# Two decoder layers on one core: memory queries produced in columns, their sums of squares on the tensor engine, and a last product cut in two

## The chip, the cores and the metric

The kernel runs on one core of a Trainium2 chip. The metric is the device time of one execution in microseconds; the time of a kernel is the median of several runs. The core's engines are named as in the profile: PE multiplies matrices, PEld is PE's loading of its stationary operand, DVE and ACT do elementwise work and reductions, POOL is a slower engine for small work, SP issues DMAs. PE writes only into PSUM, eight banks of 512 fp32 columns by 128 partitions; ACT and DVE carry results from there to SBUF.

## What is computed

Two layers over 256 positions of width 1024. With `h = RMSNorm(x)`, each layer multiplies `h` by one 1024 x 5120 matrix whose columns feed three branches and a gate:

```python
q_a, k_a, v_a, q_h, f_h, i_h, q_m, z = jnp.split(proj, split_points, axis=-1)
...
kv_m = rms_norm(mem, mem_norm_g[l]) @ w_mem_kv[l]
...
qm = rms_norm(q_m.reshape(B, S, MEM_HEADS, MEM_HEAD_DIM), mem_q_norm[l])
o_m = memory_attention(qm, km, vm).reshape(B, S, G)
...
y = jnp.concatenate([o_a, o_h, o_m], axis=-1) * jax.nn.silu(z)
x = x + y @ w_out[l]
```

Branch A is causal softmax attention (8 heads of 64), branch H a gated linear recurrence (4 heads of 128), branch M attention of the 256 positions to 256 memory tokens (4 heads of 128). The change is in branch M's queries `q_m`: each head's 128 channels are normalised by their root mean square before the scores with the memory keys.

## The kernel before

Weights come in chunks of 128 x 1024 fp32 (512 KB), one DMA each on SP. Each chunk is split in two reduced-precision parts, `wh` (a cast on ACT, L143) and `wl` (the rest, a subtraction on DVE, L158); activations are split likewise (`hTh`, `hTl`). Each product is then three matmuls: high by high, and the two mixed ones.

The projection goes column group by column group of 512. There are two forms. `group_b` (L204) holds 128 positions of the normalised input stationary and moves 512 weight columns: the result has positions on partitions and channels along the row; it is 8 x 2 x 3 = 48 matmuls of 512 columns into two PSUM tiles. `group_a` (L263) holds 128 weight columns stationary and moves the 256 positions: the result is transposed, channels on partitions and positions along the row; it is 4 x 8 x 3 = 96 matmuls of 256 columns, two of the four column blocks sharing a PSUM tile. A layer does the memory keys and values (`group_kv`), then FH and QH (`group_a`), KA, QA, IH, ZH (`group_b`), ZA and ZM (`group_a`), QM and VA (`group_b`), and then the output projection (`w_out_phase`), whose 12 row blocks of 24 matmuls are taken in the order H, A, M.

In `group_kv`, and in ZH's group in layer 0 alone, the very last matmul of 512 columns is issued as one of 384 and one of 128 (`pieces`, L215).

Everything else is written as generators that run beside this stream: `slot` (L189) steps all of them once, eight times per group, and what they emit mixes with the projection's matmuls. The final order on each engine comes from a scheduler that simulates the program when it is built; instructions handed to `pin` (L119) keep their program order on their engine, and `tc.issue_after` puts an instruction behind a named one. PSUM holds four `acc` tiles for the projections and four `sd` tiles for the generators; `held`, `room`, `take` and `rel` (L61 to L82) count who holds which buffer.

`g_qm` (L1132) takes QM's two tiles (positions on partitions): ACT copies them to `qm` (L1136) and squares them, DVE sums the squares of each head along the row (`sumsq`, L588); `rsq` (L593) makes the reciprocal roots `r` on DVE and POOL, and L1141 their negative `nr`. Then, for each half of the positions, four transposes on PE (L1150) turn the queries to channels on partitions, and ACT and DVE split them into `qmh` and `qml` (L1151, L1152). Two `g_mem_unit`s follow, two heads each: scores into two `sd` tiles (L1171), maxima on DVE, exponentials on ACT with bias `nr` times the maximum and scale `r` (L1186), division on DVE, transposes (L1205), products with the values, and the gated result for the output projection.

`g_moba_unit` (L1030) is branch A, two units a layer. After its exponentials (L1076) and the division, the three column blocks of `P` are transposed, four heads each (L1095), into three `sd` tiles, and copied to `PT` by ACT (L1096). The blocks go in the order 0, 1, 2; block 0 needs only the first half of the positions. When both units are there and VA is done, L1116 multiplies by the values.

The host lays the weights out in the order of the chunks: groups of `group_a` by column blocks, the others by row blocks (`tiles`, L1346).

Of the kernel before, what the change touches and what calls it, by code (L numbers as in the profile page):

```python
# [12 lines left out]
F32 = mybir.dt.float32  # L13
# [5 lines left out]
OP = mybir.AluOpType  # L19
# [27 lines left out]
def hymba_kernel(ctx: ExitStack, tc: tile.TileContext, front, x, x_t, mem, mem_t, positions, w_in, w_out, w_mem_kv,  # L47
# [57 lines left out]
    for l in range(DEPTH):  # L105
# [3 lines left out]
        for c in (KA, QA, IH, ZH, ZA, ZM, QM, VA):  # L109
            (add_a if c in (ZA, ZM) else add_b)(w_in, base + c * G * D)  # L110
# [86 lines left out]
    def mm(o, a, b, s, e):  # L197
        nc.tensor.matmul(o, lhsT=a, rhs=b, start=s, stop=e)  # L198
# [64 lines left out]
    def group_a(thl, each):  # L263

        for h in range(4):
# [4 lines left out]
            for k in range(8):  # L270
# [3 lines left out]
                mm(o, wL, thl[:, k, 0], False, k == 7)  # L274
                if k == 3:
                    slot(False)
            st["c"] += 1
# [378 lines left out]

    lbs = cst.tile([128, 2, 4], F32, name="lbs")
# [299 lines left out]
    def g_qk(l, q, acc):  # L957
# [41 lines left out]
        if q:  # L999
            k2 = [sb.tile([128, n], F32R, name="k2", tag=t, bufs=1)[:, n - 2048 - o:n - o].rearrange(  # L1000
                "p (h c s) -> p h c s", h=4, c=2) for t, n, o in (("k2", 2112, 48 * l), ("y2", 2048, 0))]
# [28 lines left out]
    def g_moba_unit(l, u):  # L1030
# [57 lines left out]
        yield from take(tag)  # L1088
        PT = sb.tile([128, 4, 384], F32, name="PT", tag=tag, bufs=1)
        for b in range(3):  # L1090
# [3 lines left out]
            for i in (3, 2, 1, 0):  # L1094
                pin(nc.tensor.transpose(pt[:, i * 128:(i + 1) * 128], P[:, i, bs], ident))  # L1095
# [3 lines left out]
        T[f"PT{u}"] = PT  # L1099
        if u == 0:  # L1100
            return
# [30 lines left out]
    def g_qm(l, acc):  # L1132
        ss = small("ssq", 8)
        qm = sb.tile([128, 2, 512], F32, name="qm", tag="qk", bufs=1)
        for t in range(2):
            nc.scalar.copy(qm[:, t], acc[t])  # L1136
        for t in range(2):
            sumsq(ss[:, t * 4:t * 4 + 4], acc[t], 4)
# [3 lines left out]
        yield 2  # L1142
        qmh = sb.tile([128, 4, 256], F32R, name="qmh", tag="ih", bufs=1)
        qml = sb.tile([128, 1088], F32R, name="qml", tag="hF", bufs=1)[:, 16:1040].rearrange("p (k s) -> p k s", k=4)
        for t in range(2):
            ts = slice(t * 128, (t + 1) * 128)
            yield from room("sd")
            pt = side_tile()
            for h in range(4):
                nc.tensor.transpose(pt[:, h * 128:(h + 1) * 128], qm[:, t, h * 128:(h + 1) * 128], ident)  # L1150
            nc.scalar.copy(qmh[:, :, ts], heads(pt, 4))  # L1151
            nc.vector.tensor_tensor(qml[:, :, ts], heads(pt, 4), qmh[:, :, ts].bitcast(F32), op=OP.subtract)  # L1152
            rel()
# [236 lines left out]
```

## Time and profile before

| | |
|---|---|
| median of 3 runs | 394.92 us (394.49 to 395.57) |
| the profiled execution's own time | 395.92 us |
| its span, first to last instruction | 394.1 us |
| mean granted TensorE clock | 0.999 |
| moved from and to HBM | 67.27 MB read, 1.05 MB written |
| transposes of the memory queries (L1150) | 16, two runs of four in each layer |
| transposes of branch A (L1095) | 48, 12 for each of 4 units |

The span is what the trace covers; the time of an execution holds it and a little around it. A timeline line gives the start in us, the length in us, the engine, the source line, the operation, what it writes and reads, the shapes, and how many neighbours of one kind were merged into it (x). Matmuls overlap: the length of one reaches into the next, so the distance from one start to the next is what one takes. A line can be a helper's: all plain matmuls are L198, all pinned narrow ones L202.

### The profile page before, as it was taken

The page shows a single profiled execution, that of the slowest core. Times are in us where ns is not written, and L with a number is a line of the kernel's source. Part 1 is how long each engine was busy: PE and PEld are TensorE (multiplying, and loading weights), DVE is VectorE, ACT ScalarE, POOL GpSimd, SP SyncE. Part 2 cuts the span into 40 slices and gives each one's busy share as a digit, 9 for nine tenths or more (in the row PEclk, how much of TensorE's full clock was granted, in tenths as well). Part 3 has the DMA queues.
Part 4 walks back from the last instruction along what each step waited for, and adds up shares of the span by engine and source line. Part 5 has one row for each costly group of instructions (what it writes and reads, how often), then busy time and mean ns, then how long its engine had stood idle before and what let it go on. Part 6 is the DMA issues. An engine that isn't in the chain of part 4 may idle for free.

```text
span 394.1 us, 7915 instructions
## 1 busy us (share of the span) xinstructions
PE 389.2 (99%) x3053; PEld 352.3 (89%) x3053; DVE 314.8 (80%) x632; ACT 255.9 (65%) x411; POOL 68.1 (17%) x94
## 2 busy tenths in 40 slices
PE   8999999999999999999999999999999999999996
PEld 5889988888999888999988999888889998899996
DVE  3799989999895777876586999799999684588563
ACT  5878867438757999644463876445685974968330
POOL 2005925531001002000061030033400200200000
PEclk9999999999999999999999999999999999999999
DMA  8988664549754363533656375636674266444203
GB/s 261 419 337 278 217 215 148 174 124 236 191 200 161 108 224 116 172 129 108 201 171 198 133 229 192 215 108 215 190 221 153 80 190 204 143 159 161 76 33 108
DMA packets 22662, 70.93 MB, mean 180 GB/s; under 512 B 2528, under 2 KB 5984, under 8 KB 22624
## 3 DMA queue, kind: packets, MB, share of 16 engines
q1 hardware_dynamic: 19872, 67.86, 52.3%
q10 hardware_dynamic: 2752, 2.56, 2.7%
q8 instruction: 24, 0.39, 0.4%
q14 instruction: 14, 0.11, 0.1%
HBM read 67.27 MB, written 1.05 MB: 173 GB/s over the span
## 4 chain that ended last, share of the span: by engine, by line
PE 97%; DMA 2%; SPq 0%; ACT 0%; issue 0%; DVE 0%; DVEq 0%
PE acc L198 61%; PE acc L1243 17%; PE sd L198 11%; PE sd L202 2%; DMA mw<-in_front_dram 2%; PE sd L1116 1%; PE sd L1095 1%; PE sd L1010 1%; PE sd L1205 1%; PE sd L1150 0%; PE sd L771 0%; PE sd L635 0%; SPq L123 0%; PE sd L424 0%; ACT wh L148 0%; ACT mTh L351 0%
## 5 line engine op out<-in xcount | busy, mean ns | idle before, releaser
L143 ACT CAST wh<-wr 128x1024 fp32r<-128x1024 f32 x104 | 108.7, 1052 | 72.3 <-PE acc L198 40.1
L158 DVE TENSOR_TENSOR wl<-wr,wh 128x1024 fp32r<-128x1024 f32 x104 | 126.2, 1219 | 24.2 <-PE acc L1243 8.0
L198 PE MATMUL acc<-wh,hT 128*128 128x512 f32 x385 | 121.1, 392 | 0.0
L198 PE MATMUL acc<-hT,wh 128*128 128x256 f32 x512 | 89.7, 278 | 0.0
L198 PEld LDWEIGHTS acc<-wh,hT 128*128 128x128 f32 x385 | 72.0, 188 | 14.7
L198 PEld LDWEIGHTS acc<-hT,wh 128*128 128x128 f32 x512 | 77.6, 188 | 0.2
L198 PE MATMUL acc<-wl,hT 128*128 128x512 f32 x192 | 75.5, 393 | 0.0
L198 PE MATMUL acc<-hT,wl 128*128 128x256 f32 x256 | 70.6, 278 | 0.0
L198 PEld LDWEIGHTS acc<-hT,wl 128*128 128x128 f32 x256 | 47.9, 188 | 0.0
L198 PEld LDWEIGHTS acc<-wl,hT 128*128 128x128 f32 x192 | 36.1, 188 | 7.0
L1243 PE MATMUL acc<-yh,wl 128*128 128x256 f32 x128 | 35.6, 279 | 0.0
L1243 PE MATMUL acc<-yl,wh 128*128 128x256 f32 x128 | 35.3, 277 | 0.0
L1243 PE MATMUL acc<-yh,wh 128*128 128x256 f32 x128 | 35.0, 279 | 0.0
L1243 PEld LDWEIGHTS acc<-yl,wh 128*128 128x128 f32 x128 | 24.1, 188 | 0.1
L1243 PEld LDWEIGHTS acc<-yh,wl 128*128 128x128 f32 x128 | 24.1, 188 | 0.0
L161 DVE SCALAR_TENSOR_TENSOR wl<-wr,gT,wh 128x1024 fp32r<-128x1024 f32 (+1 forms) x14 | 19.1, 1374 | 6.0 <-PE acc L1243 1.9
L1243 PEld LDWEIGHTS acc<-yh,wh 128*128 128x128 f32 x128 | 23.8, 188 | 0.1
L148 ACT ACTIVATE wh<-wr,gT 128x1024 fp32r<-128x1024 f32 (+1 forms) x14 | 15.2, 1089 | 11.4 <-PE acc L198 5.1
L1243 PE MATMUL acc<-y,wh 128*128 128x256 f32 x128 | 21.8, 276 | 0.0
L1243 PEld LDWEIGHTS acc<-y,wh 128*128 128x128 f32 x128 | 19.2, 188 | 0.0
L1243 PE MATMUL acc<-y,wl 128*128 128x256 f32 x64 | 17.5, 276 | 0.0
L1076 ACT ACTIVATE P<-P,nba,rq 128x128 f32<-128x128 f32 (+1 forms) x32 | 17.2, 540 | 0.1
(250 smaller groups left out, 675.0 us busy)
## 6 DMA issues: line engine op xcount, KB each, us to landing
wr<-in_w_in_dram SPq DMA_DIRECT2D x80, 512.0 KB, 3.7
wr<-in_w_out_dram SPq DMA_DIRECT2D x24, 512.0 KB, 3.5
wr<-in_w_mem_kv_dram SPq DMA_DIRECT2D x12, 512.0 KB, 3.3
k<-k ACTq DMA_DIRECT2D x8, 256.0 KB, 6.3
zT<-in_x_dram SPq DMA_DIRECT2D x2, 512.0 KB, 9.1
xs<-in_x_t_dram SPq DMA_DIRECT2D x2, 512.0 KB, 9.8
memr<-in_mem_dram SPq DMA_DIRECT2D x2, 512.0 KB, 5.3
mw<-in_front_dram SPq DMA_DIRECT2D x2, 384.0 KB, 6.3
```

Source lines behind the costliest of these rows:

```text
L143: ins = nc.scalar.copy(whs[i], raws[i])
L148: nc.scalar.activation(whs[i][:, sl], raws[i][:, sl], AF.Copy, scale=gT[:, g:g + 1])
L158: nc.vector.tensor_tensor(wls[i], raws[i], whs[i].bitcast(F32), op=OP.subtract)
L161: nc.vector.scalar_tensor_tensor(wls[i][:, sl], in0=raws[i][:, sl], scalar=gT[:, g:g + 1], in1=whs[i][:, sl].bitcast(F32), op0=OP.mult, op ...
L198: nc.tensor.matmul(o, lhsT=a, rhs=b, start=s, stop=e)
L202: tc.keep_in_program_order(nc.tensor.matmul(o, lhsT=a, rhs=b, start=True, stop=True))
L1010: nc.tensor.transpose(pt[:, p * 128:(p + 1) * 128], kr[:, t, p * 128:(p + 1) * 128], ident)
L1076: pin(nc.scalar.activation(P[:, i, kc[t]], P[:, i, kc[t]], AF.Exp, bias=nb[:, c:c + 1], scale=rq[:, r:r + 1], accum_out=sm[:, c:c + 1]))
L1095: pin(nc.tensor.transpose(pt[:, i * 128:(i + 1) * 128], P[:, i, bs], ident))
L1116: pin(nc.tensor.matmul(po[w][rows, c + o:c + 256], lhsT=va[:, b, h * 64:(h + 1) * 64], rhs=PT[e][:, p, 256 * b:256 + 128 * b], start=b == ...
L1205: nc.tensor.transpose(pt[:, i * 256 + t * 128:i * 256 + (t + 1) * 128], P[:, t, i, b * 128:(b + 1) * 128], ident)
L1243: ins = nc.tensor.matmul(a, lhsT=wt, rhs=y, start=first and (to is not None or b % 2 == 0), stop=n == nk - 1 and j == 2, skip_group_check= ...
```

## The change

It has four parts. The memory queries' projection (QM) goes through `group_a` instead of `group_b`, in both layers, so they arrive with channels on partitions: the eight transposes are gone, `qmh` and `qml` are written straight from the projection's tiles, and the host lays QM's weights out as for `group_a`. The sums of squares now run over partitions and are made on PE: `ones32`, 128 x 32 ones, is the stationary operand, and four products, one for each 32 positions of a half, fill the four quarters of the partitions of an `sd` tile, for each pair of heads. DVE multiplies by `m32`, which keeps of each 32 equal rows' columns the own position, and sums, so that the result has positions on partitions, as before. These products wait until the second unit of branch A has emitted its transposes.

In `g_moba_unit` the blocks are transposed in the order 1, 2, 0; in layer 0 the first unit waits until the third column block of QM's group has been issued, and its transposes stay behind that block's last matmul (`T["last"]`). The transposes of the memory units (L1205) are pinned.

The split of the last 512-column matmul in 384 and 128 applies to ZH's and VA's groups of both layers. And the tile `k2` has the same place in its buffer in both layers.

```diff
         for c in (KA, QA, IH, ZH, ZA, ZM, QM, VA):
-            (add_a if c in (ZA, ZM) else add_b)(w_in, base + c * G * D)
+            (add_a if c in (ZA, ZM, QM) else add_b)(w_in, base + c * G * D)
...
-    def group_a(thl, each):
+    def group_a(thl, each, name=None):
...
-                mm(o, wL, thl[:, k, 0], False, k == 7)
+                last = nc.tensor.matmul(o, lhsT=wL, rhs=thl[:, k, 0], start=False, stop=k == 7)
                 if k == 3:
                     slot(False)
+            T["last"] = last.ins
+            done.add((name, h))
...
+    m32 = cst.tile([128, 32], F32, name="m32")
+    ones32 = cst.tile([128, 32], F32, name="ones32")
+
+    def g_m32():
+        nc.vector.memset(ones32, 1.0)
+        nc.vector.tensor_reduce(m32, ident.rearrange("p (g s) -> p s g", g=4), AX.X, OP.add)
         yield
...
             k2 = [sb.tile([128, n], F32R, name="k2", tag=t, bufs=1)[:, n - 2048 - o:n - o].rearrange(
-                "p (h c s) -> p h c s", h=4, c=2) for t, n, o in (("k2", 2112, 48 * l), ("y2", 2048, 0))]
+                "p (h c s) -> p h c s", h=4, c=2) for t, n, o in (("k2", 2112, 0), ("y2", 2048, 0))]
...
         yield from take(tag)
+        while u == l == 0 and ("qm0", 2) not in done:
+            yield
         PT = sb.tile([128, 4, 384], F32, name="PT", tag=tag, bufs=1)
-        for b in range(3):
+        for b in (1, 2, 0):
...
             for i in (3, 2, 1, 0):
-                pin(nc.tensor.transpose(pt[:, i * 128:(i + 1) * 128], P[:, i, bs], ident))
+                with tc.issue_after(T["last"]) if u == l == 0 else nullcontext():
+                    pin(nc.tensor.transpose(pt[:, i * 128:(i + 1) * 128], P[:, i, bs], ident))
...
+        done.add(("pt", 2 * l + u))
...
-    def g_qm(l, acc):
+    def g_qm(l, h0, acc):
+        if h0 == 0:
+            T["qm"] = (sb.tile([128, 4, 256], F32R, name="qmh", tag="ih", bufs=1),
+                       sb.tile([128, 1088], F32R, name="qml", tag="hF", bufs=1)[:, 16:1040].rearrange(
+                           "p (k s) -> p k s", k=4))
+            T["q2"] = []
+        qmh, qml = T["qm"]
+        hs, a = slice(h0, h0 + 2), heads(acc, 2)
+        nc.scalar.copy(qmh[:, hs], a)
+        sq = sb.tile([128, 512], F32, name="sq", tag="sq", bufs=2)
+        nc.scalar.activation(sq, acc, AF.Square)
+        T["q2"].append(sq.rearrange("p (h t g s) -> p h t g s", h=2, t=2, g=4))
+        nc.vector.tensor_tensor(qml[:, hs], a, qmh[:, hs].bitcast(F32), op=OP.subtract)
+        if h0 == 0:
+            return
+        while ("pt", 2 * l + 1) not in done:
+            yield
+        yield from room("sd")
+        pt = side_tile()
+        for u, sq in reversed(list(enumerate(T.pop("q2")))):
+            for g in range(4):
+                mm_row(pt[g * 32:g * 32 + 32, u * 128:u * 128 + 128], ones32, sq[:, :, :, g])
         ss = small("ssq", 8)
-        qm = sb.tile([128, 2, 512], F32, name="qm", tag="qk", bufs=1)
-        for t in range(2):
-            nc.scalar.copy(qm[:, t], acc[t])
-        for t in range(2):
-            sumsq(ss[:, t * 4:t * 4 + 4], acc[t], 4)
+        sd = sb.tile([128, 512], F32, name="sq", tag="sq", bufs=2)[:, :256]
+        nc.vector.tensor_tensor(sd.rearrange("p (a s) -> p a s", s=32), pt[:, :256].rearrange("p (a s) -> p a s", s=32),
+                                m32[:, None, :].to_broadcast([128, 8, 32]), op=OP.mult)
+        nc.vector.tensor_reduce(ss.rearrange("p (t h) -> p h t", t=2), sd.rearrange("p (h t s) -> p h t s", t=2, s=32),
+                                AX.X, OP.add)
+        rel()
         r = rsq("qm", ss, 8, 128)
         nr = small("nrm", 8)
         nc.gpsimd.tensor_scalar(nr, r, -1.0, None, op0=OP.mult)
-        yield 2
-        qmh = sb.tile([128, 4, 256], F32R, name="qmh", tag="ih", bufs=1)
-        qml = sb.tile([128, 1088], F32R, name="qml", tag="hF", bufs=1)[:, 16:1040].rearrange("p (k s) -> p k s", k=4)
-        for t in range(2):
-            ts = slice(t * 128, (t + 1) * 128)
-            yield from room("sd")
-            pt = side_tile()
-            for h in range(4):
-                nc.tensor.transpose(pt[:, h * 128:(h + 1) * 128], qm[:, t, h * 128:(h + 1) * 128], ident)
-            nc.scalar.copy(qmh[:, :, ts], heads(pt, 4))
-            nc.vector.tensor_tensor(qml[:, :, ts], heads(pt, 4), qmh[:, :, ts].bitcast(F32), op=OP.subtract)
-            rel()
         yield 2
...
-                    nc.tensor.transpose(pt[:, i * 256 + t * 128:i * 256 + (t + 1) * 128],
-                                        P[:, t, i, b * 128:(b + 1) * 128], ident)
+                    pin(nc.tensor.transpose(pt[:, i * 256 + t * 128:i * 256 + (t + 1) * 128],
+                                            P[:, t, i, b * 128:(b + 1) * 128], ident))
...
+    spawn(g_m32(), 40)
...
+            elif gen is g_qm:
+                group_a(hT, lambda h, a: g_qm(l, h, a), f"qm{l}")
             else:
-                acc = group_b(hTh, hTl, gen is g_zh and not l)
+                acc = group_b(hTh, hTl, gen in (g_zh, g_va))
...
-            if c in (FH, QH, ZA, ZM):
+            if c in (FH, QH, ZA, ZM, QM):
```

More of the change, by code (lines that the diff above doesn't have):

```diff
@@ L1129, in g_moba @@
             yield 4
-    def g_qm(l, acc):
-        ss = small("ssq", 8)
-        qm = sb.tile([128, 2, 512], F32, name="qm", tag="qk", bufs=1)
-        for t in range(2):
-            nc.scalar.copy(qm[:, t], acc[t])
-        for t in range(2):
-            sumsq(ss[:, t * 4:t * 4 + 4], acc[t], 4)
+    def g_qm(l, h0, acc):
[14 more added lines that the diff above has]
+        while ("pt", 2 * l + 1) not in done:
+            yield
+        yield from room("sd")
[3 more added lines that the diff above has]
+                mm_row(pt[g * 32:g * 32 + 32, u * 128:u * 128 + 128], ones32, sq[:, :, :, g])
+        ss = small("ssq", 8)
+        sd = sb.tile([128, 512], F32, name="sq", tag="sq", bufs=2)[:, :256]
[4 more added lines that the diff above has]
+        rel()
         r = rsq("qm", ss, 8, 128)
```

## The prediction

> **What bounds the kernel now.** I read the page first: busy time by engine, then the chain that ended last, then the timeline of PE around the places that the change touches.
>
> ```profile
> PE 389.2 (99%) x3053; PEld 352.3 (89%) x3053; DVE 314.8 (80%) x632; ACT 255.9 (65%) x411; POOL 68.1 (17%) x94
> ...
> PE 97%; DMA 2%; SPq 0%; ACT 0%; issue 0%; DVE 0%; DVEq 0%
> ```
>
> PE is busy for 389.2 of 394.1 us, and 97% of the chain is PE following PE. So the time is a sum of what each PE instruction costs. Busy PE is not proof of a full PE, so I price an instruction by the distance from its start to the next start, in the timeline (start us, us, engine, line, what). First the two products that carry the kernel, 512 columns and 256 columns wide, where nothing interrupts them:
>
> ```profile
> 330.36 0.62 PE L198 MATMUL acc<-wh,hT 128*128 128x512 f32 x2
> ...
> 331.04 0.62 PE L198 MATMUL acc<-wh,hT 128*128 128x512 f32 x2
> ...
> 374.04 0.28 PE L1243 MATMUL acc<-yl,wh 128*128 128x256 f32 x1
> ...
> 374.38 0.28 PE L1243 MATMUL acc<-yl,wh 128*128 128x256 f32 x1
> ```
>
> Three 512s start between 330.36 and 331.04, 0.68 us, 0.227 each; three 256s between 374.04 and 374.38, 0.34 us, 0.113 each. Two 256s cost one 512.
>
> **The change part by part.** (1) *The projection of the memory queries.* Before: 48 products of 512 columns, 48 x 0.227 = 10.9 us a layer. After: 4 x 8 x 3 = 96 products of 256 columns, 96 x 0.1134 = 10.9 us. Nothing is gained or lost in the product itself; its four weight loads stay four DMAs of 512 KB on SP, cast by ACT and split by DVE as before.
>
> A rule of the Trainium skill speaks against this part: the page "TensorE: Matmul & The Clock Gate", section "Back-to-back issue gap", gives 262 cycles for 256 columns and 518 for 512. By it, 96 x 262 - 48 x 518 = 288 cycles would be an estimated 0.12 us more a layer at that page's 2.4 GHz, and the sum below 0.24 us worse. The rows here do not agree: 2 x 0.113 is 0.227 to their last digit.
>
> (2) *Eight transposes a layer go (L1150).* The columns come out of the product with the head's channels on partitions already. Layer 1 shows them cleanly:
>
> ```profile
> 338.99 0.60 PE L1150 MATMUL sd<-ident,qm 128*128 128x128 f32 x4
> ...
> 342.66 0.60 PE L1150 MATMUL sd<-ident,qm 128*128 128x128 f32 x4
> ...
> 346.55 0.28 PE L1243 MATMUL acc<-yh,wh 128*128 128x256 f32 x1
> ```
>
> Between the first and second run lie 14 products of 512 columns, between the second and the first product of the output projection 15. 342.66 - 338.99 - 14 x 0.2267 = 0.50, and 346.55 - 342.66 - 15 x 0.2267 = 0.49. So a run of four costs 0.49 us with all that it does to the products behind it. Four runs in two layers: **-1.96 us**.
>
> (3) *Sums of squares on PE come in.* Sums over a head's 128 channels now run across partitions: eight products a layer, 128x32 ones as weights, 128 columns moving, four of them side by side in the array, so two groups of four. No row shows this shape. The nearest are the 32-wide rows of the linear recurrence:
>
> ```profile
> 70.72 0.84 PE L198 MATMUL acc<-wh,hT 128*128 128x512 f32 x3
> 71.49 1.57 PE L202 MATMUL sd<-hQ,hK 128*32 128x48 f32 x128
> 72.98 0.50 PE L198 MATMUL acc<-wl,hT 128*128 128x512 f32 x1
> ...
> 73.56 0.39 PE L198 MATMUL acc<-wl,hT 128*128 128x512 f32 x1
> ...
> 83.32 0.61 PE L198 MATMUL acc<-wh,hT 128*128 128x512 f32 x2
> 83.86 0.89 PE L202 MATMUL sd<-hQ,hK 128*32 128x48 f32 x64
> 84.68 1.09 PE L1010 MATMUL sd<-ident,kr 128*128 128x128 f32 x8
> 85.53 0.48 PE L198 MATMUL acc<-wl,hT 128*128 128x512 f32 x1
> ...
> 86.08 0.40 PE L198 MATMUL acc<-wl,hT 128*128 128x512 f32 x1
> ```
>
> From 70.72 to 73.56 start five 512s (three, one, and one left out): 2.84 - 1.13 = 1.71 us for 32 groups of four. From 83.32 to 86.08 start four: 2.76 - 0.91 - 0.87 for the eight transposes (part 4) = 0.98 us for 16 groups. The difference, 0.73 for 16 groups, is 0.045 a group, and 0.98 - 16 x 0.045 = 0.26 us is the price of going into this mode and out again; standing alone it is 1.71 - 32 x 0.045 = 0.27. A group grows with its columns: 0.045 x 128/48 = 0.12. So 2 x 0.12 + 0.26 = **0.50 us a layer, +1.0 us**. The lower end lets a group cost 0.045 whatever its width: 0.35. The upper end takes the columns one after another, as the 64-wide products do:
>
> ```profile
> 166.68 2.87 PE L1116 MATMUL sd<-PT,va 128*64 128x256 f32 x32
> 169.49 1.09 PE L1205 MATMUL sd<-ident,P 128*128 128x128 f32 x8
> ```
>
> 32 products, half of 256 and half of 128 columns (6144 in all), take 2.81 us, 0.457 ns a column; 8 x 128 columns would be 0.47, and with 0.26 the sums 0.73. I take 0.50 because its row has the same four-abreast form.
>
> (4) *Runs of twelve.* The attention transposes (L1095) stand in runs of four and eight now:
>
> ```profile
> 137.59 1.03 PE L1095 MATMUL sd<-ident,P 128*128 128x128 f32 x8
> 138.46 0.60 PE L771 MATMUL sd<-ident,zh 128*128 128x128 f32 x4
> 138.82 0.71 PE L198 MATMUL acc<-wh,hT 128*128 128x512 f32 x2
> 139.36 0.40 PE L198 MATMUL acc<-wl,hT 128*128 128x512 f32 x1
> ...
> 156.08 1.03 PE L1095 MATMUL sd<-ident,P 128*128 128x128 f32 x8
> 156.87 0.36 PE L1243 MATMUL acc<-yh,wh 128*128 128x256 f32 x1
> 157.07 0.28 PE L1243 MATMUL acc<-yl,wh 128*128 128x256 f32 x1
> ```
>
> Here already stand twelve in one run: 139.36 - 137.59 - 2 x 0.227 = 1.32. Eight cost 157.07 - 156.08 - 0.12 = 0.87. So a transpose costs 0.11 in a run of any length; against 0.87 + 0.49 = 1.36 twelve in one save up to 0.04. I take half, since a run of twelve has a tail of its own that 1.32 does not count; four runs: **-0.08 us**. Pinning L1205's transposes adds none.
>
> (5) *The last product in two pieces*, newly in layer 1's ZH and both VA groups. The one place that has it, and then products of 256 columns behind transposes and behind an unsplit 512:
>
> ```profile
> 101.01 0.40 PE L198 MATMUL acc<-wh,hT 128*128 128x384 f32 x2
> 101.24 0.33 PE L198 MATMUL acc<-hT,wl 128*128 128x256 f32 x1
> ...
> 101.66 0.28 PE L198 MATMUL acc<-hT,wl 128*128 128x256 f32 x1
> ...
> 320.82 0.28 PE L198 MATMUL acc<-hT,wl 128*128 128x256 f32 x1
> ...
> 323.64 0.28 PE L198 MATMUL acc<-hT,wl 128*128 128x256 f32 x1
> ...
> 346.67 0.28 PE L1243 MATMUL acc<-yl,wh 128*128 128x256 f32 x1
> ...
> 347.37 0.28 PE L1243 MATMUL acc<-yl,wh 128*128 128x256 f32 x1
> ```
>
> The two pieces and three 256s (one, and two left out) take 0.65 where 0.227 + 3 x 0.113 = 0.57 would do: the cut costs 0.08. What it may buy is the pace behind it. Six 256s behind an unsplit group take 347.37 - 346.67 = 0.70, 0.117 each; 24 behind a transpose run take 2.82, 0.1175 each; undisturbed it is 0.113. I call that the slow pace, 0.004 us a product. A cut that restores the pace for some 20 products wins back its 0.08. I put the part at 0, between +0.24 (three cuts, no gain) and -0.2 (pace restored over 40 products each). The same pace is a risk of part 1: 192 products of 256 columns now stand where 512s did, and if all ran slow behind the twelve, that were +0.8; I put it at 0 as well.
>
> *What hides the rest.* Two copies of the queries fall away on ACT, which is full where they stand:
>
> ```profile
> 129.20:141.00 11.80, 11.80 (x63) 9.95 (x62) 10.17 (x23) 11.76 (x24) 0.00 (x0) 1.00 0.35 117
> 141.00:154.20 13.20, 13.20 (x65) 10.91 (x64) 8.86 (x18) 13.17 (x29) 2.38 (x2) 1.00 0.59 203
> ...
> 149.61 1.64 POOL L597 TENSOR_TENSOR qmr<-qmm,pw 128x8 f32<-128x8 f32 x1 [22.61 <-DVE qmm L595]
> 151.33 0.74 POOL L1141 TENSOR_SCALAR nrm<-qmr 128x8 f32<-128x8 f32 x1
> ...
> 156.64 1.55 ACT L1096 COPY PT<-sd 128x512 f32<-128x512 f32 x3
> ...
> 161.05 0.15 DVE L1180 TENSOR_TENSOR nbm<-mxm,nrm 128x4 f32<-128x4 f32 x1
> ```
>
> (stretch, then busy us of PE, PEld, DVE, ACT, POOL). ACT has 11.76 of 11.80 and 13.17 of 13.20 us full while PE never waits, so fewer copies only add cover. What becomes late is the scale of the memory queries: its sums wait for the second unit's twelve, whose last now starts before 156.87. Then come a DVE product and reduction, 1.64 and 0.74 us on POOL: some 4 us, so the bias of the exponentials (161.05) comes at about 161.5 to 163. Behind that bias on ACT queue the weight casts; the transposes that need the result stand at 169.49. The memory branch's rows of the output projection are the last 96 of its 288 products, so 192 x 0.113 = 21.8 us of PE's own work stand behind 154.2, where it starts, before they are due. A slip of 2 us is covered; without that cover each microsecond late were one of PE, in each layer. The mask of ones (one memset, one reduction on DVE, once) lies under PE from the start.
>
> **Sum**, against the profiled execution's own span of 394.1 us (its time, 395.92 us, holds 1.8 us around the span): -1.96 + 1.0 - 0.08 + 0 = -1.04. The median of the three runs, 394.92 us, is 1.0 below the profiled time; a change in PE's work carries over unscaled, so 394.92 - 1.04 = **393.9 us**, -0.26%.
>
> **Rivals.** *Cheap sums, kept pace.* If a group of sums costs 0.045 to 0.08 and the cuts restore the pace, it is -1.96 + 0.75 - 0.08 - 0.2 = -1.5: 393.4 us. For it: four abreast, steps of 0.045. Against: their columns are 2.7 times as many. *The run waits for banks.* Twelve transposes and the sums take four "sd" banks in a row, pinned in order on PE; if ACT hasn't emptied the third or fourth, every product behind them stands, the weight buffers stay taken, and with them SP's loads. Three copies that empty such banks (L1096) take 1.55 us, 0.52 each. If each of the four runs finds two copies undone, that is +4.1 - 1.04 = 398.0 us; it decides from 2.2 us in all, about one copy a run, where slower by 0.3% begins. For it: ACT is full just there. Against it: the runs of eight and of twelve above show no such hole, and with two copies fewer a layer ACT is less full. *The order is not what the words say*: the scheduler puts the twelve in three runs of four. Then each costs 3 x 0.49 - 1.32 = 0.15 more, +0.6 in all, 394.5 us; within no change. *Four passes.* Plain fp32 products repeat: 8 x 128 columns x 0.457 ns x 4 = 1.87 + 0.26 a layer, +4.3 - 2.04 = 397.2 us. Against it: L1116's products are of plain fp32 tiles and show one pass. In the Trainium skill, "FP8 and Floating Point Precision", section "TensorE Precision Notes", counts four passes for true fp32; those rows do not agree.
>
> **How the numbers follow.** About 0.3% (1.2 us) is what a measurement of this kernel can tell from no change. Forecast, with the split order, -0.4 to -1.2 us, and what lies up to the upper end of the range: 0.48. Cheap sums, over 1.2 us faster: 0.42, near because the forecast stands 0.14 us short of that bound. Bank waits 0.08, four passes 0.02: slower, 0.10. The range takes the cheap end, 393.1 (sums 0.35, cuts at their best), and at the other the dear sums (+0.46) with the slow pace throughout (+0.8), 395.2.
>
> **What would show it.** Right: no L1150; L202 rows of 128x32 straight behind twelve L1095, about 0.5 us from the last transpose's end to the pace regained; 96 QM products at 0.113. Wrong: a hole in front of a transpose run, 256s at 0.117 through QM, sums over 0.7.

## The result, and the profile after

The changed kernel takes 397.34 us (median of 6 runs, 397.08 to 397.66), the kernel before 394.83 us (6 runs beside them, 394.49 to 395.57). The ratio is 1.0058, with a 95% interval of 1.0048 to 1.0069: 2.5 us slower, where 393.9 us was forecast and 393.1 to 395.2 allowed.

The two profiled executions lie only 1.2 us apart (397.08 and 395.92 us). The one of before had a wait at its very start that the one of after does not have. In the timeline of PE (start us, us, engine, line, what; in brackets the idle time and what ended it) before shows

```profile
7.90 0.62 PE L198 MATMUL acc<-wl,mTh 128*128 128x512 f32 x2
9.15 0.50 PE L198 MATMUL sd<-wh,mTh 128*128 128x512 f32 x1 [0.64 <-ACT wh L148]
```

and after, at the same two places,

```profile
7.89 0.61 PE L198 MATMUL acc<-wl,mTh 128*128 128x512 f32 x2
8.35 0.39 PE L198 MATMUL sd<-wh,mTh 128*128 128x512 f32 x1
```

Two products of 512 columns need 0.45 us, so PE was ready at 8.35 in both, and before stood 0.80 us. Without it the profiles differ by 2.0 us. That is what has to be found. The rest up to 2.5 lies within the spread of single runs, 1.1 us for before.

The page of after shows no new bound, only more of the same: PE is as full as before, with 115 more records on it.

```profile
PE 390.4 (99%) x3168; PEld 357.7 (91%) x3168; DVE 315.3 (80%) x634; ACT 254.6 (64%) x407; POOL 66.9 (17%) x94
...
PE 96%; DVE 1%; DMA 1%; ACT 0%; issue 0%; SPq 0%; DVEq 0%
```

DVE has 1% of the chain where it had 0%. Everything else must be in what a PE instruction costs, so I went through the timeline of PE stage by stage (in after, L1095's old transposes are L1108, L1205's are L1229, the output projection is L1267, the values' products L1130).

**The projection of the memory queries** came out as forecast. Right behind layer 0's run of twelve:

```profile
139.53 0.39 PE L198 MATMUL acc<-hT,wh 128*128 128x256 f32 x2
...
141.91 0.40 PE L198 MATMUL acc<-wh,hT 128*128 128x512 f32 x1
```

Between the two starts lie 21 products of 256 columns: 2.38 / 21 = 0.113 us. The slow pace does not touch them.

**The run of twelve and the sums**, once without sums (layer 1, first unit) and once with them (second unit):

```profile
317.78 1.48 PE L1108 MATMUL sd<-ident,P 128*128 128x128 f32 x12
319.09 0.49 PE L781 MATMUL sd<-ident,zh 128*128 128x128 f32 x3
...
347.47 1.47 PE L1108 MATMUL sd<-ident,P 128*128 128x128 f32 x12
348.88 0.64 PE L202 MATMUL sd<-sq,ones 128*32 128x128 f32 x16
349.45 0.39 PE L1267 MATMUL acc<-yh,wh 128*128 128x256 f32 x1
349.68 0.28 PE L1267 MATMUL acc<-yl,wh 128*128 128x256 f32 x1
```

Twelve transposes take 1.31 us up to a further transpose. A product starts 0.08 sooner behind the last of them, so twelve take 1.23 up to a product (that is also what e5_hole and e11_half show below); that product's step is then 0.20 instead of 0.113 (171.14 to 171.34 below). Twelve and the sums take 1.98 up to the first product, whose step is 0.23. So the sums cost 1.98 - 1.23 + 0.03 = 0.78 us a layer, 0.57 of them between their first start and the next product's. Note the count: the code issues eight products, the trace has 16 rows.

**A hole** stands in layer 0's first run of twelve:

```profile
137.28 1.04 PE L1108 MATMUL sd<-ident,P 128*128 128x128 f32 x8
138.68 0.66 PE L1108 MATMUL sd<-ident,P 128*128 128x128 f32 x4 [0.36 <-DVE yl L785]
139.09 0.49 PE L198 MATMUL acc<-hT,wh 128*128 128x256 f32 x2
```

From 137.28 to 139.09 are 1.81 us where 1.23 would do: 0.58 us. The third bank is still held by the gate's transposes, which DVE's L785 empties, and DVE's timeline shows why that is late:

```profile
134.07 0.20 DVE L1091 RECIPROCAL ria<-sma 128x8 f32<-128x8 f32 x1 [1.59 <-ACT P L1086]
...
136.75 1.22 DVE L158 TENSOR_TENSOR wl<-wr,wh 128x1024 fp32r<-128x1024 f32 x1
137.88 0.74 DVE L785 SCALAR_TENSOR_TENSOR yl<-sd,gT,yh 128x512 fp32r<-128x512 f32 x1
```

The eight scalings of the attention weights follow the reciprocal, then the gate's product and the split of a weight, and only then L785. The whole row starts late: DVE stood 1.59 us before the reciprocal, until ACT had made the last exponentials (L1086).

**The output projection lost its pace.** The windows view gives the same two stretches of both kernels (stretch, then busy us of PE, PEld, DVE, ACT, POOL with the records that touch the stretch, granted clock, DMA share, GB/s). Before:

```profile
184.00:198.00 14.00, 14.00 (x126) 14.00 (x125) 7.55 (x8) 5.68 (x6) 0.47 (x1) 1.00 0.56 188
376.00:388.00 12.00, 12.00 (x109) 12.00 (x108) 5.57 (x8) 2.37 (x3) 0.00 (x0) 1.00 0.04 12
```

After:

```profile
184.00:198.00 14.00, 14.00 (x121) 14.00 (x120) 7.97 (x9) 6.19 (x7) 0.22 (x1) 1.00 0.50 169
376.00:388.00 12.00, 12.00 (x105) 12.00 (x104) 5.55 (x7) 2.62 (x3) 0.00 (x0) 1.00 0.01 2
```

Some two of the counted products hang over the edges, so it is about 14.0 / 124 = 0.113 us before and 14.0 / 119 = 0.118 after. PE is full and its clock granted at 1.00 in both. Step by step, the slow pace begins right behind each of the memory branch's two runs of transposes and lasts up to the next disturbance: 45 products behind the first run, some 178 behind the second, in each layer, up to the next layer's 512-column products or the end. In before it let go 5 products behind the first run and 12 behind the second. 2 x 223 products of 0.0045 us are 2.0 us, against 0.15 in before: **+1.9 us**. Where these runs stand is different too. After:

```profile
166.06 2.87 PE L1130 MATMUL sd<-PT,va 128*64 128x256 f32 x32
168.86 0.39 PE L1267 MATMUL acc<-yh,wh 128*128 128x256 f32 x1
...
170.35 1.04 PE L1229 MATMUL sd<-ident,P 128*128 128x128 f32 x8
171.14 0.36 PE L1267 MATMUL acc<-yh,wh 128*128 128x256 f32 x1
171.34 0.28 PE L1267 MATMUL acc<-yl,wh 128*128 128x256 f32 x1
...
176.90 1.03 PE L1229 MATMUL sd<-ident,P 128*128 128x128 f32 x8
177.69 0.36 PE L1267 MATMUL acc<-yh,wh 128*128 128x256 f32 x1
```

Twelve products of the projection stand between the values' products and the first run, and the second run too has products of the projection on both sides. Before, the first run followed the values' products directly (its rows stand in the prediction), and the second stood within the memory branch's own products:

```profile
174.43 0.28 PE L198 MATMUL sd<-PTh,vmh 128*128 128x256 f32 x1
174.55 1.03 PE L1205 MATMUL sd<-ident,P 128*128 128x128 f32 x8
175.34 0.36 PE L198 MATMUL sd<-PTl,vmh 128*128 128x256 f32 x1
```

The sum, then: eight transposes a layer gone, -1.96 as forecast; runs of twelve, -0.08; sums, 2 x 0.78 = +1.56; the hole, +0.58; the pace, +1.9. Together +2.0, as much as was found.

### The profile page after: what moved, and what is told of

The parts are those of the page before. It is cut to its first block, busy times and chain, and to the rows that moved or that the text cites. A ratio compares the mean times of both kernels' runs of the same rounds, so it can differ in the third digit from the quotient of the medians.

```text
span 395.2 us, 8142 instructions
## 1 busy us (share of the span) xinstructions
PE 390.4 (99%) x3168; PEld 357.7 (91%) x3168; DVE 315.3 (80%) x634; ACT 254.6 (64%) x407; POOL 66.9 (17%) x94
## 4 chain that ended last, share of the span: by engine, by line
PE 96%; DVE 1%; DMA 1%; ACT 0%; issue 0%; SPq 0%; DVEq 0%
PE acc L198 51%; PE acc L1267 17%; PE sd L198 11%; PE acc L274 9%; PE sd L202 2%; PE sd L1130 1%; PE sd L1108 1%; DMA wr<-in_front_dram 1%; PE sd L1020 1%; PE sd L1229 1%; PE sd L637 0%; DVE P L1095 0%; PE sd L781 0%; SPq L123 0%; DVE yl L785 0%
## 5 line engine op out<-in xcount | busy, mean ns | idle before, releaser
L198 PE MATMUL acc<-hT,wh 128*128 128x256 f32 x640 | 111.8, 278 | 0.0
L198 PE MATMUL acc<-wh,hT 128*128 128x512 f32 x324 | 100.5, 388 | 0.0
L198 PEld LDWEIGHTS acc<-hT,wh 128*128 128x128 f32 x640 | 96.7, 188 | 0.1
L274 PE MATMUL acc<-hT,wl 128*128 128x256 f32 x320 | 88.1, 277 | 0.0
L198 PEld LDWEIGHTS acc<-wh,hT 128*128 128x128 f32 x324 | 60.8, 188 | 12.5
L198 PE MATMUL acc<-wl,hT 128*128 128x512 f32 x160 | 62.9, 393 | 0.0
L274 PEld LDWEIGHTS acc<-hT,wl 128*128 128x128 f32 x320 | 59.9, 188 | 0.0
L1267 PE MATMUL acc<-yh,wh 128*128 128x256 f32 x128 | 36.6, 286 | 0.0
L1267 PE MATMUL acc<-yl,wh 128*128 128x256 f32 x128 | 35.7, 279 | 0.0
L1267 PE MATMUL acc<-yh,wl 128*128 128x256 f32 x128 | 35.4, 279 | 0.0
L198 PEld LDWEIGHTS acc<-wl,hT 128*128 128x128 f32 x160 | 30.0, 188 | 5.9
L1267 PEld LDWEIGHTS acc<-yh,wh 128*128 128x128 f32 x128 | 24.0, 188 | 0.7 <-issue 0.5
L1267 PEld LDWEIGHTS acc<-yl,wh 128*128 128x128 f32 x128 | 24.3, 190 | 0.0
L1267 PEld LDWEIGHTS acc<-yh,wl 128*128 128x128 f32 x128 | 24.0, 188 | 0.0
L1267 PE MATMUL acc<-y,wh 128*128 128x256 f32 x128 | 22.6, 281 | 0.0
L1267 PEld LDWEIGHTS acc<-y,wh 128*128 128x128 f32 x128 | 19.7, 190 | 0.0
L1267 PE MATMUL acc<-y,wl 128*128 128x256 f32 x64 | 17.8, 281 | 0.0
L1086 ACT ACTIVATE P<-P,nba,rq 128x128 f32<-128x128 f32 (+1 forms) x32 | 17.2, 540 | 0.1
```

What stands on the lines that cost most here:

```text
L274: last = nc.tensor.matmul(o, lhsT=wL, rhs=thl[:, k, 0], start=False, stop=k == 7)
L1086: pin(nc.scalar.activation(P[:, i, kc[t]], P[:, i, kc[t]], AF.Exp, bias=nb[:, c:c + 1], scale=rq[:, r:r + 1], accum_out=sm[:, c:c + 1]))
L1267: ins = nc.tensor.matmul(a, lhsT=wt, rhs=y, start=first and (to is not None or b % 2 == 0), stop=n == nk - 1 and j == 2, skip_group_check= ...
```

## The experiments

Theory A: the pace of the 256-column products has two states, 0.113 and 0.118 us. A run of transposes can throw it into the slow one, where it stays until something in the sequence of products breaks it. This makes most of the loss. Rivals: the slow pace comes from where the new tiles lie (B) or from the new cuts of the values' last product (C); or the loss lies in the new order of the attention transposes (D). Times are medians; the kernel before ran beside each group and took 394.84 to 395.10.

**Break the order of the operands, add nothing** (e1_swap).

```diff
-            for j, (wt, y) in enumerate(((wH, yh), (wH, yl), (wL, yh))):
+            terms = ((wH, yl), (wH, yh), (wL, yh)) if (n, b) == (6, 0) else ((wH, yh), (wH, yl), (wL, yh))
+            for j, (wt, y) in enumerate(terms):
```

> The changed kernel, but in the output projection's products the three terms of one triple (n = 6, first block of columns) of each layer stand in the order wH*yl, wH*yh, wL*yh. No instruction is added. Theory A (the pace of the 256-column products is a state that locks behind a run of transposes and lasts until the regular sequence is broken; in the changed kernel it stays at 0.118 us instead of 0.113 over some 200 products a layer): the break lets the pace go back behind n = 6, so 0.6 to 1.0 us a layer are won, 395.3 to 396.1 us. Theory B (the slow pace comes from where the operands lie in SBUF): same as the changed kernel, 397.3, and the steps stay at 0.118 to the end. Theory C (the pace has its cause in the cuts of the values' product): also 397.3.

396.97 us, ratio to before 1.0054 (1.0040 to 1.0068). The steps stay at 0.118 to the end of both layers, where theory A had expected this break to free them. What is read and in which order does not free the pace.

**Undo the order of the attention transposes** (e2_order).

```diff
-        while u == l == 0 and ("qm0", 2) not in done:
-            yield
-        for b in (1, 2, 0):
+        for b in range(3):
...
-                with tc.issue_after(T["last"]) if u == l == 0 else nullcontext():
+                with nullcontext():
```

> The changed kernel with the blocks of the attention transposes in the order 0, 1, 2 again, and without the wait of layer 0's first unit for the memory queries' second group, so that its twelve need not stand in one run. The hole theory (a step of 630 ns within the run of twelve of layer 0's first unit, where the third bank was not yet empty): the hole of 0.5 us goes and a run of its own of four transposes comes back at 0.13 at most: 396.8 to 397.0 us. If the hole is only moved to the place where the run of eight stands: 397.3. Theory A of the pace makes no claim here, except that the output projection stays at 0.118 if the place of its transposes in the order does not move.

399.55 us, 1.0121 (1.0107 to 1.0134): 2.2 us worse than the changed kernel, against both expectations. The timeline of PE says why:

```profile
133.44 0.39 PE L198 MATMUL acc<-hT,wh 128*128 128x256 f32 x2
135.03 0.65 PE L1106 MATMUL sd<-ident,P 128*128 128x128 f32 x4 [1.20 <-DVE P L1095]
```

Four transposes stand in PE's order ahead of data that DVE has not scaled yet, and PE stands 1.4 us. The pace is slow in more places as well: over 83 products behind the sums in each layer, where the changed kernel has some 20, and in layer 1 through the whole projection of the memory queries. So the new order and the wait, taken back together here, earn their place together, and rival D falls: the output projection is slow with the old order too.

**Leave the new cuts out** (e3_nocut).

```diff
-                acc = group_b(hTh, hTl, gen in (g_zh, g_va))
+                acc = group_b(hTh, hTl, gen is g_zh and not l)
```

> The changed kernel without the new cuts (the last 512-column product whole again in both groups of the attention's values and in layer 1's gate). Theory C (the cuts set the phase with which the output projection goes into its slow pace): the projection goes back to 0.113 behind its transposes, -1.9 us, 395.4. Theory A: the pace behind the values' products stays slow up to the next transposes (some 30 products of 0.004 each, +0.1 a place, against a cut of 0.08), and the output projection stays at 0.118 unless chance frees it: 397.0 to 397.6.

397.00 us, 1.0053 (1.0040 to 1.0065), the projection at 0.118 as before. Rival C falls; the cuts are worth nothing that can be measured.

**Cut one product of the projection** (e4_kick).

```diff
-                    ins = nc.tensor.matmul(a, lhsT=wt, rhs=y, ...
+                    for q in ((slice(0, 128), slice(128, 256)) if (n, b, j) == (6, 0, 2) else (slice(0, w),)):
+                        ins = nc.tensor.matmul(a[:, q], lhsT=wt, rhs=y[:, q], ...
```

> The changed kernel, but one product of the output projection (n = 6, first block of columns, last of its three terms) of each layer is made in two pieces of 128 columns. It adds 0.06 to 0.1 us a layer by itself. Theory A (a locked pace that a break in the sequence frees): steps of 0.113 behind the cut, -0.6 to -1.0 us a layer less the cut, 395.5 to 396.4 us. Theory B (place of the operands in SBUF) and theory C (the cuts of the values): no change of the pace, 397.4 to 397.6.

395.98 us, 1.0032 (1.0019 to 1.0044): 1.4 us faster than the changed kernel, with one product more in each layer. Around the cut, and in the two stretches of above:

```profile
180.67 0.28 PE L1268 MATMUL acc<-yh,wh 128*128 128x256 f32 x1
180.79 0.28 PE L1268 MATMUL acc<-yl,wh 128*128 128x256 f32 x1
180.90 0.33 PE L1268 MATMUL acc<-yh,wl 128*128 128x128 f32 x2
181.07 0.33 PE L1268 MATMUL acc<-yh,wh 128*128 128x256 f32 x1
181.25 0.28 PE L1268 MATMUL acc<-yl,wh 128*128 128x256 f32 x1
181.36 0.28 PE L1268 MATMUL acc<-yh,wl 128*128 128x256 f32 x1
```

```profile
184.00:198.00 14.00, 14.00 (x126) 14.00 (x125) 8.40 (x9) 6.21 (x7) 0.61 (x1) 1.00 0.51 173
376.00:388.00 12.00, 12.00 (x109) 12.00 (x108) 6.19 (x8) 2.62 (x3) 0.00 (x0) 1.00 0.03 11
```

126 and 109 records again, as in before. The tiles lie where they lay, so rival B falls. 152 and 150 products won back 0.0045 us each, 1.36 us, less some 0.12 for each cut and the steps behind it: 1.1, which is what the trace gains on that of the changed kernel from the first cut to the end.

**Cut right behind each run** (e6_kicks: the condition of e4_kick reads `(n, b, j) in ((3, 4, 2), (5, 0, 2))`).

> The changed kernel with a product in two halves as in e4_kick, but right behind each run of the memory branch's transposes (third product behind it: n = 3, fifth block of columns, and n = 5, first block), so twice a layer. If a pair of short products frees the pace wherever it stands: some 45 and 177 products of 0.0045 each go back to 0.113, 1.0 us a layer, less 2 x 0.12 for the two cuts and what follows them: 397.3 - 1.5 = 395.8, a little under e4_kick's 395.98. If it frees the pace only when it stands far from the transposes (a phase that has to settle first): 397.6, no better than the changed kernel.

395.79 us, 1.0018 (1.0010 to 1.0027). The pace is back at 0.113 within five products behind all four cuts. So it needs no time to settle.

**The same cut in the kernel before, where the pace is fast** (e8_ctl: e4_kick's edit in the kernel before).

> The kernel before with the same single product in two halves as in e4_kick (n = 6, first block of columns). There the output projection already runs at 0.113 at that place, so theory A expects only the cost of the cut and of the steps behind it, 0.06 to 0.12 us a layer: 395.0 to 395.1. A rival, that cutting a product wins something by itself whatever the pace: 394.2 or less.

395.34 against 394.99 us, 1.0010 (1.0000 to 1.0021). A cut wins nothing by itself; if anything it costs.

**Move the memory branch's transposes back** (e10_near; in the generator of a memory unit, ahead of its transposes).

```diff
                 nc.vector.tensor_scalar(P[:, t, i], P[:, t, i], ri[:, c:c + 1], None, op0=OP.mult)
-        yield 2
         yield from take("PTh", "PTl")
```

> The changed kernel without the pause ahead of the memory branch's transposes, so that the first run of eight stands directly behind the values' products, as in the kernel before (n = 3, first block), and the second at n = 4, behind 110 of the 288 products, within a triple. Place theory (a run of these transposes locks the slow pace where products of the output projection stand on both sides of it, and does not where it follows the values' products directly): behind the first run the steps are back at 0.113 after some 5 products, in both layers, which wins 0.2 us a layer; behind the second nothing is promised, as it has products on both sides: 396.9 if it locks, 395.3 if it does not (in the kernel before the second run stood within the memory branch's own products and let go after 11). Rival (the lock comes from the change's pins or tiles wherever the runs stand): both stay slow, 397.3.

395.33 us, 1.0011 (1.0001 to 1.0021): 2.0 us of the 2.5 are gone. The first run stands directly behind the values' products, the second directly behind the memory branch's; behind both the steps are fast within 5 products, in both layers.

```profile
166.28 2.87 PE L1130 MATMUL sd<-PT,va 128*64 128x256 f32 x32
169.08 1.09 PE L1228 MATMUL sd<-ident,P 128*128 128x128 f32 x8
169.93 0.37 PE L1266 MATMUL acc<-yh,wh 128*128 128x256 f32 x1
...
175.66 0.28 PE L198 MATMUL sd<-PTh,vmh 128*128 128x256 f32 x1
175.78 1.03 PE L1228 MATMUL sd<-ident,P 128*128 128x128 f32 x8
176.57 0.37 PE L1266 MATMUL acc<-yh,wl 128*128 128x256 f32 x1
```

**Move them alone, in the kernel before** (e14_far).

```diff
-        yield 2
+        yield 5
         yield from take("PTh", "PTl")
...
-                    nc.tensor.transpose(pt[:, i * 256 + t * 128:i * 256 + (t + 1) * 128],
-                                        P[:, t, i, b * 128:(b + 1) * 128], ident)
+                    pin(nc.tensor.transpose(pt[:, i * 256 + t * 128:i * 256 + (t + 1) * 128],
+                                            P[:, t, i, b * 128:(b + 1) * 128], ident))
```

> The kernel BEFORE with one thing of the change's effects alone: the memory branch's two runs of eight transposes moved to where they stand in the changed kernel (a longer pause ahead of them, and kept in program order; n = 3, fifth block, and n = 5, first block, behind 84 and 120 of the 288 products). Place theory: the output projection goes into the slow pace behind both, 45 and 178 products of 0.0045 us a layer, 2.0 us in two layers less the 0.1 that the old second run cost: 396.9 us. If something else of the change (its tiles, its sums, its cuts) has to come with it: 395.0, steps back at 0.113 within some 12 products.

396.78 against 394.95 us, 1.0048 (1.0035 to 1.0061). The kernel before, with nothing of the change but the place of sixteen transposes a layer and their pins, is 1.8 us slower, and its projection runs as in the changed kernel:

```profile
184.00:198.00 14.00, 14.00 (x121) 14.00 (x120) 8.04 (x9) 6.30 (x8) 0.81 (x1) 1.00 0.44 154
376.00:388.00 12.00, 12.00 (x104) 12.00 (x103) 5.85 (x7) 2.62 (x3) 0.00 (x0) 1.00 0.01 1
```

In e10_near the transposes are pinned as well and the pace is fast, so the pins don't make it. The two runs show the largest term from both sides: it comes and goes with the place of these runs. What it is about the place they don't show (e13_nearb, below, has a run at e10_near's place and the slow pace behind it).

**The sums in one pass** (e7_sumb; the squares are rounded to 8 bits).

```diff
-    ones32 = cst.tile([128, 32], F32, name="ones32")
+    ones32 = cst.tile([128, 32], mybir.dt.bfloat16, name="ones32")
...
-        sq = sb.tile([128, 512], F32, name="sq", tag="sq", bufs=2)
+        sq = sb.tile([128, 512], mybir.dt.bfloat16, name="sq", tag="sq", bufs=2)
```

> The changed kernel with the squares and the ones of the sums in bf16 (the squares are rounded to 8 bits), so that each of the eight products is one instruction on PE instead of two. Two-pass theory (a product of plain fp32 is carried out as two, which the prediction missed): the sums' body falls from 0.574 to about 0.29 us a layer, -0.6 us in all: 396.7. Rival (what costs is the way into the 32-wide form and out of it, or the columns whatever their type): 397.3.

396.48 us, 1.0036 (1.0024 to 1.0049), 0.86 less than the changed kernel. The eight products are eight rows now, and the next product starts 0.23 us behind their first (155.346 to 155.573) where it was 0.57:

```profile
155.35 0.30 PE L202 MATMUL sd<-sq,ones 128*32 128x128 bf16 x8
155.57 0.39 PE L1268 MATMUL acc<-yh,wh 128*128 128x256 f32 x1
```

**Give the third bank more time** (e5_hole: the first unit waits for `("qm0", 3)`, 24 products later; e11_half: group_a reports a group at its half, and the unit waits for the fourth one's, 12 products later).

> The changed kernel, but layer 0's first unit waits for the fourth group of the memory queries before its run of twelve, in place of the third, so the run stands 24 products (2.8 us) later and the third bank, which the gate's DVE product empties, is free by then. Bank theory (the step of 630 ns in the run is a wait for a bank): the step falls to about 110 ns and the time by 0.5 us, to 396.8. Rival (the step comes from the twelve themselves, a price of a long run): the step stays and the time is 397.3. The twelve of the other three runs have no such step, which speaks for the bank.

> The changed kernel, with the first unit's run of twelve 12 products (1.36 us) later: after half of the memory queries' fourth group, where e5_hole had it after all of it and lost on ACT what it won at the bank. If the slack of ACT is more than 1.4 us: the step of 630 ns in the run falls to 110 and no product waits later, 396.8. If ACT has no slack there: the run shows no hole, and the wait comes back some 12 us later, in front of the second unit's transposes or in front of the cast of a weight: 397.2 to 397.6.

e5_hole took 398.17 us (1.0082, 1.0067 to 1.0096), e11_half 397.12 us (1.0055, 1.0042 to 1.0067). In both the run of twelve has no hole, 1.23 us; in both PE stands elsewhere instead, and neither came down to the 396.8 us of the bank theory. In e5_hole three times (its profiled execution took 399.56 us, more than the others, with longer waits at its very start besides):

```profile
139.02 0.39 PE L274 MATMUL acc<-hT,wl 128*128 128x256 f32 x1 [0.34 <-DVE wl L158]
...
154.64 0.39 PE L1267 MATMUL acc<-yh,wh 128*128 128x256 f32 x1 [0.60 <-ACT wh L143]
...
155.90 0.55 PE L1108 MATMUL sd<-ident,P 128*128 128x128 f32 x3 [0.52 <-DVE P L1095]
```

and in e11_half once:

```profile
138.21 0.38 PE L274 MATMUL acc<-hT,wl 128*128 128x256 f32 x1 [0.35 <-DVE wl L158]
```

The hole was not the bank's alone. DVE is half a microsecond late at 138: if PE does not meet it at the bank, it meets it at the split of the next weight. With the run 2.8 us later, as in e5_hole, ACT is late too for what follows (the cast at 154.64).

**Take work off DVE there** (e15_pool: four of the first unit's eight scalings of P, 768 columns, on POOL; e17_pool3: three of them, 512 columns).

> The changed kernel, but in layer 0's first unit half of the eight scalings of the attention weights (every second head, 768 of 1536 columns) run on POOL instead of DVE. POOL is idle there; its 128x512 products take 1.69 us, so 768 columns some 2.5 us beside DVE's own 1 us, done at 136.8, before the run of twelve at 137.3. Theory (the hole of 0.5 us in the run of twelve and its moved forms in e5_hole and e11_half are one lateness of DVE at 134 to 139): DVE is 0.9 us ahead, the hole goes and nothing takes its place: 396.8. Rival (POOL's scalings become late, or DVE waits for something else): 397.3 or more, with the hole at the first transposes instead.

> e15_pool with 512 instead of 768 columns on POOL, which took 4.03 us for 768 and was late by 0.7: 2.7 us, done 0.6 us ahead of the run of twelve, while DVE gains some 0.5 us. Theory (one lateness of DVE): no step above 300 ns within the run or ahead of it, -0.5: 396.8. Rival (what DVE gains it loses again, or POOL is late again): 397.3.

e15_pool took 397.50 us (1.0061, 1.0048 to 1.0075): the step within the run is gone and no weight is late, but POOL needs 4.03 us where I had worked out 2.5, and the run starts late:

```profile
138.02 1.53 PE L1109 MATMUL sd<-ident,P 128*128 128x128 f32 x12 [1.02 <-POOL P L1095]
```

e17_pool3 took 396.57 us (1.0048, 1.0036 to 1.0061). POOL is in time, DVE's L785 starts 3.65 us behind the reciprocal that opens the scalings instead of 3.81 (137.19 - 133.54, in the changed kernel 137.88 - 134.07), and the idle time in the run falls by the same 0.16, from 0.36 to 0.20. The hole was expected to close, and most of it stayed:

```profile
137.99 0.66 PE L1109 MATMUL sd<-ident,P 128*128 128x128 f32 x4 [0.20 <-DVE yl L785]
```

DVE's lateness is the cause, as far as these go: what it gains comes off the hole. In both runs DVE stands the same 1.59 us for ACT's exponentials before the reciprocal; no run takes that wait away, so whether it is the root of the lateness stays open. The time of e17_pool3 is 0.8 below the changed kernel's, but the two intervals overlap; between the traces the rest of the difference is a shorter wait at the very start (0.14 us for 0.57), which the edit doesn't touch.

**All remedies together.** e12_best has e6_kicks, e7_sumb and e11_half; e13_nearb has e10_near and e7_sumb; e16_best2 and e18_best3 are e13_nearb with the scalings of e15_pool and of e17_pool3.

> The changed kernel with the halved products of e6_kicks, the sums in bf16 of e7_sumb (squares rounded to 8 bits) and the half step of e11_half. If the three add up: 397.3 - 1.55 - 0.86 - 0.5 = 394.4, which is 0.5 below the kernel before. If the hole comes back elsewhere: 394.9, the same as before.

> The changed kernel with e10_near's place of the memory branch's transposes and e7_sumb's sums in bf16 (squares rounded to 8 bits). If the two add up: 395.3 - 0.86 = 394.5, some 0.5 below the kernel before (395.0). If the shorter sums move the second run back between products of the output projection: 395.3 or more.

> e13_nearb (transposes of the memory branch directly behind the values' products, sums in bf16) with e15_pool's scalings on POOL. If the hole goes: 394.92 - 0.5 = 394.4, some 0.5 below the kernel before. If not: 394.9, the same as before.

> e13_nearb (transposes of the memory branch directly behind the values' products, sums in bf16) with e17_pool3's three scalings on POOL: 394.92 - 0.5 = 394.4 if the hole goes, 0.5 below the kernel before; 394.9 if it stays.

They took 395.26 (1.0010, 0.9998 to 1.0021), 394.92 (1.0001, 0.9993 to 1.0010), 395.96 (1.0020, 1.0011 to 1.0029) and 394.70 us (0.9997, 0.9984 to 1.0011). None can be told from before on the fast side, and none reached the 394.4 or 394.5 that the sum of its parts promised. In e16_best2 the run of twelve stands 1.02 us for POOL's scalings, as in e15_pool. The trace of e13_nearb names one part of its miss: the first run, directly behind the values' products as in e10_near, was followed by 30 slow products there, 0.13 us in each layer. So that place is no guarantee: the same neighbours gave the fast pace in e10_near and, with nothing but shorter sums ahead of them, the slow one here.

## Why the prediction was wrong

1. *Eight transposes a layer go, -1.96.* They are gone. No run priced them alone; with 1.96 the terms add up to what was found.
2. *The projection of the queries costs the same.* Right: 0.113 us a product.
3. *The sums, 0.50 us a layer.* The mechanism was right, the size was not: 0.78, above the 0.73 of the upper end and above the 0.7 named as a sign of being wrong. The mistake is a count. I read the rows of the 32-wide products as instructions of the code and took 128 rows for 32 groups of four. The code issues 64 there: a product of plain fp32 leaves two rows. So a group costs 0.09 instead of 0.045, at 128 columns 0.24 instead of 0.12, and 2 x 0.24 + 0.26 = 0.74 would have been the forecast. e7_sumb shows it from the other side: 0.23 us in bf16 for the 0.57. The same misreading is in the argument against four passes: L1116's 32 rows come from 16 products, two abreast, so 3072 columns and not 6144 take the 2.81 us, and one product alone would have 1.83 ns a column, four times the 0.113 / 256 = 0.44 of the projection's. The Trainium skill ("FP8 and Floating Point Precision", "TensorE Precision Notes") has four passes for true fp32; the times here fit it, and the rows that the prediction held against it do not speak against it. The sums still cost far less than that rival's 1.87 + 0.26 us a layer, because four of them run abreast: 1.87 / 4 + 0.26 would have been 0.73.
4. *Runs of twelve, -0.08.* Right where nothing waits: 1.23 us and 0.09 in the step behind them, the 1.32 of the prediction; and all four stand in one run, so the rival of a split order did not come.
5. *The pace, put at 0.* This is the step that failed, and the largest miss. I had seen both paces and asked what they would do to the products that the change brings in, with +0.8 us at the far end. Those stayed fast (in e2_order, in layer 1, they did not). The products that slowed down were ones the change does not touch, because the transposes between them stand 12 products later in the built order: +1.9 us where the sum had 0. That the place of these runs brings the slow pace is what e14_far and e10_near show.
6. *The slip of the chain is covered.* As a wait it was: the bias of the exponentials came at 160.51 us, earlier than the 161.5 to 163 that I gave it; the 161.05 of before, without the 0.80 us at its start, would be 160.25. But in this kernel the order is laid out by counting pauses when it is built, and the memory units are spawned behind the sums, which wait for the second unit's twelve. That this is what moved the transposes by 12 products is read from the code; that one pause less moves them back is e10_near.
7. *The rival of the banks.* It came true at one of four runs, at about the price given for one copy (0.58 us for 0.52), and not quite for the reason given: the bank waits for DVE's L785, not for a copy on ACT, though DVE itself had stood 1.59 us for ACT. It was to decide from 2.2 us on and did not by itself.
8. *The cuts, between +0.24 and -0.2.* Right: nothing measurable (e3_nocut).

## What to carry to other kernels

When PE is full, also look at the order of what a change does not touch: a run of small transposes that lands some products later can cost more than the instructions removed. Where a stream of equal products runs 4% slow behind such a run, try the run behind another kind of product (e13_nearb: it doesn't always help), or cut one product in two, and compare the count of products in equal stretches. Before pricing an operation by a row, count how many rows one instruction of the code leaves.

## What was not expected of the hardware

The 256-column product has two steady paces, 0.113 and 0.118 us, with PE full, the granted clock at 1.00 and no wait in either. In the eleven kernels shown here in which the memory branch's transposes have the projection's products on both sides and no cut follows at once, the slow pace followed each of the four runs, and held over up to some 179 products. In the kernels with these runs behind other products it let go after 3 to 12, but for the 30 products behind the first run in e13_nearb and the two kernels built on it. Swapping operands does not break it; two products of 128 columns do, wherever they stood. The 512-column products behind it always came back to 0.227 within about five. The Trainium skill ("TensorE: Matmul & The Clock Gate", "Back-to-back issue gap") gives as the isolated gap of a product its columns at 2.4 GHz and 2.5 ns, an estimated 0.109 us for 256; neither pace here is that. What holds the slow pace stays open; the traces show only starts and modelled ends.

POOL took 4.03 us to scale 768 columns by a scalar per partition in e15_pool and 2.29 us for 512 in e17_pool3; DVE did the other 768 of e15_pool in 1.28. That POOL was so late shows on PE, which stood for it in e15_pool.
